# First tile of a split-GELU multiply: two contiguous blocks of four adjacent rows a partition

## Chip, cores, metric

One core of one Trainium2 chip. The metric is the device time of one execution in microseconds (us). Before: 469.24 us, median of 3 runs (469.23 to 469.35).

## The reference

```python
def setup_inputs():
    batch, seq, dim = (32, 512, 2048)
    return {'x': np.random.randn(batch, seq, dim).astype(np.float32)}

def reference(x):
    half_dim = x.shape[-1] // 2
    x1, x2 = x[..., :half_dim], x[..., half_dim:]          # copies cut
    gelu_x1 = 0.5 * x1 * (1 + erf(x1 / np.sqrt(2)))
    return (gelu_x1 * x2).astype(np.float32)
```

That is 16,384 rows of 8 KiB in and of 4 KiB out: 134.22 MB read and 67.11 MB written.

## The kernel before

Sixteen tiles of 1024 rows. In each, a partition holds eight adjacent rows (64 KiB in, 32 KiB out). There are two input and two output buffers. SP (SyncE) issues the loads, ACT (ScalarE) does the GELU and issues most stores, DVE (VectorE) multiplies. The first tile is loaded, and the first and last tiles are stored, in two halves of four rows a partition.

```python
    R = 8
    x_t = x_flat.rearrange("(n p r) d -> n p r d", p=P, r=R)
    o_t = out_flat.rearrange("(n p r) d -> n p r d", p=P, r=R)
    # ... buffers and semaphores cut ...
    def load(i, rows, sem):
        ins = nc.sync.dma_start(out=x_bufs[i % 2][:, rows, :], in_=x_t[i][:, rows, :])
        counted(ins, sem, 16)
        return ins

    def store(queue, i, rows, sem):
        queue.wait_ge(mul_done, n[mul_done.name])
        counted(
            queue.dma_start(out=o_t[i][:, rows, :], in_=o_bufs[i % 2][:, rows, :]), sem, 16
        )

    for ins in (
        load(0, slice(0, 4), first[0]),
        load(0, slice(4, 8), first[1]),
        load(1, slice(0, 8), ready[1]),
    ):
        tc.no_tile_sem_insts.add(ins.ins.name)
    # ... for each tile i (cut): wait for its load and for the store that frees its output buffer,
    #     GELU and multiply in pieces, store, then load(i + 2)
```

## Time and profile before

| | before |
|---|---|
| time, median of 3 | 469.24 us |
| span of the profiled run | 467.9 us |
| DVE / ACT busy | 140.5 us (30%) / 115.5 us (25%) |
| two DMA queues, share of 16 engines | 70.6% + 29.1% |

The prediction below shows most of the profile lines. In addition, these are lines of the page's list of DMA issues: what is copied, the issuing queue, how often, KB each, and the median us from issue to landing.

```profile
x_tile<-in_x_dram SPq DMA_DIRECT2D x2, 4096.0 KB, 16.6
out_dram<-o_tile ACTq DMA_DIRECT2D x2, 2048.0 KB, 34.5
...
x_tile<-in_x_dram SPq DMA_DIRECT2D x15, 44.2
```

The first line is the two half loads, the second the two half stores of the first tile. The times to landing hold the waiting behind other transfers on the same sixteen DMA engines. "DMA engine" here is always one of those sixteen. The trace records each packet that they move, with start, duration and size, but not which engine moved it: a packet is put on the engine whose packet before it ends as it starts. That gives each of the sixteen the same 120 loads of 64 KiB.

### The profile page before, as it was taken

To read this page: it belongs to the slowest core of one execution; us is meant where nothing else is said; L and a number is where in the kernel's file an instruction comes from. 1 tells how busy PE (TensorE), PEld (TensorE's weight loads), DVE (VectorE), ACT (ScalarE), POOL (GpSimd) and SP (SyncE) were. 2 spreads that over 40 slices of the span, in tenths; PEclk is the share of its full clock that TensorE was granted. 3 is DMA by queue.
4 is the path that set the end of the run, shared out by engine and by line. 5 is a ranking of instruction groups with operands and counts; after the bars stand their busy time and mean duration, and the time that the engine had idled before them with its cause. 6 is when DMAs were issued, how large, how long until landed. Compare 5 with 4: busy or idle time off the path is not lost.

```text
span 467.9 us, 152 instructions
## 1 busy us (share of the span) xinstructions
DVE 140.5 (30%) x34; ACT 115.5 (25%) x35; POOL 0.2 (0%) x4
## 2 busy tenths in 40 slices
DVE  0330514207052060511606116060150702507043
ACT  1320606042060410604106050050500506014060
POOL 0000000000000000000000000000000000000000
DMA  8999999999999999999999999999999999999998
GB/s 359 448 448 443 403 405 492 409 403 448 459 437 403 434 417 493 403 403 448 476 420 403 445 406 493 403 406 445 487 409 403 445 451 448 403 434 417 493 389 373
DMA packets 5041, 201.34 MB, mean 430 GB/s; under 512 B 560, under 2 KB 560, under 8 KB 560
## 3 DMA queue, kind: packets, MB, share of 16 engines
q1 hardware_dynamic: 2880, 142.61, 70.6%
q10 hardware_dynamic: 2160, 58.72, 29.1%
q14 instruction: 1, 0.01, 0.0%
HBM read 134.22 MB, written 67.11 MB: 430 GB/s over the span
## 4 chain that ended last, share of the span: by engine, by line
DMA 76%; DVE 14%; ACT 8%; ACTq 0%; SPq 0%; issue 0%
DMA out_dram<-o_tile 66%; DVE o_tile L89 14%; DMA x_tile<-in_x_dram 10%; ACT o_tile L81 8%; ACTq L112 0%; SPq L47 0%
## 5 line engine op out<-in xcount | busy, mean ns | idle before, releaser
L89 DVE TENSOR_TENSOR o_tile<-o_tile,x_tile 128x5120 f32<-128x5120 f32 (+3 forms) x34 | 140.5, 4171 | 319.7 <-ACT o_tile L81 319.7
L81 ACT ACTIVATE o_tile<-x_tile 128x5120 f32<-128x5120 f32 (+3 forms) x34 | 114.3, 3407 | 337.4 <-DMA out_dram<-o_tile 301.6
L81 ACT ACT_TABLE_LOAD x1 | 1.3, 1283 | 2.9 <-PEq L67 2.9
L135 POOL MEMSET const-bfloat16-1.0<- 128x1 bf16 x1 | 0.1, 101 | 0.0
L135 POOL MEMSET const-uint8-127<- 128x1 uint8 x1 | 0.1, 101 | 0.0
L135 POOL MEMSET const-float32-0.0<- 128x1 f32 x1 | 0.1, 98 | 0.2 <-issue 0.2
L135 POOL MEMSET const-float32-1.0<- 128x1 f32 x1 | 0.1, 98 | 0.0
## 6 DMA issues: line engine op xcount, KB each, us to landing
out_dram<-o_tile ACTq DMA_DIRECT2D x13, 4096.0 KB, 44.7
x_tile<-in_x_dram SPq DMA_DIRECT2D x2, 4096.0 KB, 16.6
out_dram<-o_tile ACTq DMA_DIRECT2D x2, 2048.0 KB, 34.5
out_dram<-o_tile SPq DMA_DIRECT2D x1, 4096.0 KB, 25.2
out_dram<-o_tile SPq DMA_DIRECT2D x2, 2048.0 KB, 7.8
x_tile<-in_x_dram SPq DMA_DIRECT2D x15, 44.2
```

Of the source, the lines that this page charges most:

```text
L81: nc.scalar.activation(out=o_bufs[k][:, rows, :], in_=x_bufs[k][:, rows, :half], func=GELU),
L89: nc.vector.tensor_mul(out=o_bufs[k][:, rows, :], in0=o_bufs[k][:, rows, :], in1=x_bufs[k][:, rows, half:],),
L135: nc = _bacc.Bacc("TRN2", target_bir_lowering=False, num_devices=1)
```

## The change

In the old form, a half load takes every second 32 KiB of the first tile's 8 MiB, and a half store every second 16 KiB of its 4 MiB. The new form gives partition p of half h the four rows from 4p on in block h, so that each half is one contiguous piece of memory. The intent is longer contiguous runs for the transfers that stand at the kernel's start. Nothing else changes.

```diff
+    x_h = x_t[0].rearrange("p r d -> (p r) d").rearrange("(h p r) d -> h p r d", h=2, p=P)
+    o_h = o_t[0].rearrange("p r d -> (p r) d").rearrange("(h p r) d -> h p r d", h=2, p=P)
     def load(i, rows, sem):
-        ins = nc.sync.dma_start(out=x_bufs[i % 2][:, rows, :], in_=x_t[i][:, rows, :])
+        src = x_h[rows.start // 4] if i == 0 else x_t[i][:, rows, :]
+        ins = nc.sync.dma_start(out=x_bufs[i % 2][:, rows, :], in_=src)
     def store(queue, i, rows, sem):
         queue.wait_ge(mul_done, n[mul_done.name])
-        counted(
-            queue.dma_start(out=o_t[i][:, rows, :], in_=o_bufs[i % 2][:, rows, :]), sem, 16
-        )
+        dst = o_h[rows.start // 4] if i == 0 else o_t[i][:, rows, :]
+        counted(queue.dma_start(out=dst, in_=o_bufs[i % 2][:, rows, :]), sem, 16)
```

## The prediction

> **What bounds the kernel now.** I read the page first (engine shares, DMA row, queues), then the chain of work that ended last in order of time, then the table of stretches over the first 21 us, then the single DMA packets that the trace records.
>
> The page: no compute engine is busy for a third of the span, and the DMA row is full from slice 2 to slice 39.
>
> ```profile
> span 467.9 us, 152 instructions
> DVE 140.5 (30%) x34; ACT 115.5 (25%) x35; POOL 0.2 (0%) x4
> DMA  8999999999999999999999999999999999999998
> DMA packets 5041, 201.34 MB, mean 430 GB/s; under 512 B 560, under 2 KB 560, under 8 KB 560
> q1 hardware_dynamic: 2880, 142.61, 70.6%
> q10 hardware_dynamic: 2160, 58.72, 29.1%
> HBM read 134.22 MB, written 67.11 MB: 430 GB/s over the span
> ```
>
> The two queues together hold 70.6 + 29.1 = 99.7% of sixteen engines' span. There are 17 loads and 18 stores, 35 transfers; 560 = 35 x 16 packets are the tiny completion writes, so 5041 - 560 - 1 = 4480 = 35 x 128 carry data: **one packet for each partition of each transfer**. Their sizes in the packet records: on q1 384 of 32 KiB (256 of the two half loads of the first tile, the rest of one whole store), 1920 of 64 KiB (the 15 whole loads) and 256 of 16 KiB (the last tile's half stores), and on q10 256 of 16 KiB (the two half stores of the first tile) and 1664 of 32 KiB (13 whole stores).
>
> The chain of waits confirms it from the other side: 76% of it is DMA, and its pieces are a transfer of some 44.7 us, an ACT and two DVE instructions, and a transfer again. Its start is one uninterrupted load piece:
>
> ```profile
> 1.59 0.05 issue
> 1.64 45.54 DMA x_tile<-in_x_dram
> 47.18 0.02 issue
> 47.20 4.48 ACT o_tile L81
> 51.68 0.02 issue
> 51.70 8.77 DVE o_tile L89 x2
> 60.48 0.02 issue
> 60.50 40.04 DMA out_dram<-o_tile
> ```
>
> The chain shows ACT and DVE for 13.3 us of each round, but the DMA row stays at 9 during them, since the next load is queued then. So I don't take that 13.3 us for a loss: the bound is the sixteen DMA engines, from their first packet to their last.
>
> The table of stretches for the part that the change touches (start up to the first packets' end; first half load; second half load):
>
> ```profile
> core 0: us, DVE busy (x) ACT busy (x) POOL busy (x), PEclk, DMA share, GB/s
> 0.00:3.40 3.40, 0.00 (x0) 0.54 (x1) 0.20 (x4) 1.00 0.54 154
> 3.40:11.90 8.50, 0.00 (x0) 0.74 (x1) 0.00 (x0) 1.00 1.00 432
> 11.90:21.55 9.65, 4.49 (x2) 3.71 (x2) 0.00 (x0) 1.00 1.01 435
> ```
>
> The gapped half loads already run at 432 and 435 GB/s, with a DMA share of 1.00 and 1.01. There is no idle time in them to win.
>
> **What the Trainium skill says.** (1) "DMA: Bandwidth & Descriptors", section "Where 436 GB/s comes from", puts the ceiling of the sixteen ports at 435 GB/s. The trace agrees: 432 and 435 GB/s in the two half loads. (2) "Perfetto Trace Analysis", section "Contiguity and DMAs": contiguity "only matters within an SBUF partition line". In both kernels each partition gets 32 KiB in one piece from memory. The trace agrees that a gap costs nothing: the gapped 32 KiB load packets take 1213 ns (median; 27.0 GB/s on one engine), and 64 KiB packets of the whole loads, which leave no gaps, take 2418 ns (27.1 GB/s). (3) "DMA: Bandwidth & Descriptors", section "Latency and other measured facts", reports loss from power-of-two row pitches of 512 KiB and more. The change takes the load pitch from 64 KiB to 32 KiB and the store pitch from 32 to 16 KiB, all below that; no run here has such a large pitch. (4) Same page, section "Why a DMA increments its semaphore by 16 and not by 1": the number of engines comes from the slowest dimension of both patterns, 128 partitions giving 16. The trace agrees: every transfer has 16 completion writes.
>
> **The change part by part.**
>
> *Removed and added:* nothing is counted differently. Two half loads of 4 MiB, two half stores of 2 MiB, the same six ACT and DVE instructions on the same shapes, the same waits. Only DRAM addresses move: partition p of half h takes rows 4p to 4p+3 of block h in place of half of its own eight rows.
>
> *Number and size of packets:* the whole stores of the kernel before are of just the new form (128 partitions, 32 KiB each, no gaps in memory), and the packet records show 128 packets of 32 KiB for each. I take it that the new half loads become 128 packets of 32 KiB and the new half stores 128 of 16 KiB, as now.
>
> *Cost of a packet:* load, 32 KiB: starts on one engine are 1209 to 1210 ns apart, back to back. 8 packets an engine and half, 2 halves: 16 x 1.21 = 19.4 us. Store, 16 KiB: 611 ns each, 16 x 0.611 = 9.8 us. In all the change touches 29.1 us of each engine's 465 us, **6%**. To move the total by 2% (9.4 us), these packets would have to become a third faster or slower. A third faster is not to be had, as they run at the rate of all the others.
>
> *What could still change:* I chained the packets of each engine by time and added up what each took above the median of its size. Over the whole kernel this is 1.0 us an engine, and only in two places: about 0.61 us in the first packets (1596 to 1985 ns in place of 1213, starting at 1.74 to 2.30 us), and 0.33 us at 21.6 to 30 us, where the second tile's load begins (2538 to 2942 ns in place of 2418). After 50 us it is 0.00 to 0.02 in every 10 us. The first is the cold start of sixteen streams, which a contiguous source does not take away: the first packet of each engine is contiguous already. The second belongs to the next tile's load, which the change leaves alone. I give the pair an expected change of 0, with a swing of some 0.3 us either way. As the engines are backlogged from 1.74 to 467 us, any such change carries through to the end one to one.
>
> *Beside other work:* the compute of the first tile (ACT 7.3 us, DVE 8.9 us) lies wholly beside loads and keeps its landing times of about 12.7 and 22.4 us.
>
> Sum: 469.24 + 0.0 (packets) + 0.0 (compute) + 0.0 (start) = **469.2 us**.
>
> **Rivals.**
>
> *The gap in memory costs something that the change recovers* (fewer open pages, longer runs). For: the first packets are slow. Against: from the second packet on, gapped and ungapped packets have the same rate within 0.4%, and in the stretch table the half loads stand at the kernel's own ceiling. At most the 0.6 us of the cold start plus the 0.3 us of the transition could vanish: 468.3 us. Chance of more than 0.4 us gained: 6%.
>
> *The smaller pitch makes the engines collide in memory.* Sixteen engines start within 0.6 us of each other, now at half the distance in memory. If the first loads ran 10% slower, that is 1.9 us: 471.1 us. Against: whole stores go at this very pitch of 32 KiB with 1213 ns a packet. Chance of more than 0.4 us lost: 7%.
>
> *The contiguous region is cut into other descriptors or given to fewer engines* (a region with no gaps could be folded into one long run). On one engine 4 MiB would take 128 x 1.21 = 155 us, and the kernel would be well over 100 us slower; with more, smaller packets on sixteen engines, the effect would be below 1 us. Against: whole loads and whole stores are free of gaps too, and are spread over sixteen engines with one packet a partition. Chance of a visible loss: under 1%.
>
> **Range and chances.** The three runs before lie within 0.12 us. To that I add the swing of 0.3 us and a little for another chip's session: **468.9 to 469.6 us**. The rivals on either side leave about 6% below and 8% above, and somewhat more for the unknown. Faster by over 2% (under 460.0 us) has no mechanism: 0.004. Slower by over 2% (over 478.8 us) only by the third rival: 0.006. Within 2%: 0.99.
>
> **What would show each step right or wrong.** Right: 5041 packets and 201.34 MB again; 560 tiny ones; 32 KiB load packets at 1213 ns after each engine's first, and 16 KiB store packets at 611 ns; half loads landing near 12.7 and 22.4 us; 430 to 436 GB/s in the stretches 3.4 to 11.9 and 11.9 to 21.55 us; chain and waits as before. Wrong: another count of packets (third rival), 32 KiB packets over 1250 ns in the first 22 us (second rival), first packets near 1213 ns or the second tile's first packets near 2418 ns with a total of 468.3 to 468.8 us (first rival). A change of the later 44.7 us pieces would refute the claim that nothing beyond the first tile is touched.

## The result, and the profile after

Six executions of the changed kernel: 469.14, 469.29, **471.70**, 469.28, **471.37**, 469.16 us. The median is 469.28. Six of the kernel before: 469.23 to 469.35, median 469.30. The ratio is 1.0015 (95% interval 0.9991 to 1.0038). Ratios here are the mean time of one kernel's runs over that of the other's of the same rounds, so not quite the ratio of the medians. Executions over 1.5% slower than the fastest of the same kernel are left out of the means. The mean of the six is 470.0 us, as two of them took 2.2 and 2.5 us longer than the others.

The profiled execution is one of the short ones (469.14 us). Its page, the lines that answer to those of before:

```profile
span 467.8 us, 152 instructions
DMA  8999999999999999999999999999999999999988
DMA packets 5041, 201.34 MB, mean 430 GB/s; under 512 B 560, under 2 KB 560, under 8 KB 560
q1 hardware_dynamic: 2880, 142.61, 70.6%
q10 hardware_dynamic: 2160, 58.72, 29.1%
...
x_tile<-in_x_dram SPq DMA_DIRECT2D x2, 4096.0 KB, 16.9
out_dram<-o_tile ACTq DMA_DIRECT2D x2, 2048.0 KB, 34.1
...
x_tile<-in_x_dram SPq DMA_DIRECT2D x15, 44.4
```

The same packets and the same bytes. The half loads land 0.3 us later (16.9 for 16.6). Its table of stretches:

```profile
core 0: us, DVE busy (x) ACT busy (x) POOL busy (x), PEclk, DMA share, GB/s
0.00:3.40 3.40, 0.00 (x0) 0.54 (x1) 0.20 (x4) 1.00 0.56 154
3.40:11.90 8.50, 0.00 (x0) 0.74 (x1) 0.00 (x0) 1.00 1.00 432
11.90:21.55 9.65, 4.50 (x2) 3.71 (x2) 0.00 (x0) 1.00 1.01 435
```

The contiguous half loads run at 432 and 435 GB/s, to the digit as the gapped ones did (a stretch counts the packets that start in it, so a shift of some 0.1 us does not show). The start of its chain of waits:

```profile
1.64 45.34 DMA x_tile<-in_x_dram
46.99 0.02 issue
47.01 4.48 ACT o_tile L84
```

The first piece ends 0.19 us sooner (46.99 for 47.18), although the half loads landed later. So a short execution is much as predicted. It has nothing to say about the two long ones, whose traces were not kept.

### The profile page after: what moved, and what is told of

Read it like the earlier page. It is cut to its first block, busy times and chain, and to the rows that moved or that the text cites. A ratio compares the mean times of both kernels' runs of the same rounds, so it can differ in the third digit from the quotient of the medians.

```text
span 467.8 us, 152 instructions
## 1 busy us (share of the span) xinstructions
DVE 140.5 (30%) x34; ACT 115.5 (25%) x35; POOL 0.2 (0%) x4
## 2 busy tenths in 40 slices
DMA packets 5041, 201.34 MB, mean 430 GB/s; under 512 B 560, under 2 KB 560, under 8 KB 560
## 4 chain that ended last, share of the span: by engine, by line
DMA 76%; DVE 14%; ACT 8%; ACTq 0%; SPq 0%; issue 0%
DMA out_dram<-o_tile 66%; DVE o_tile L92 14%; DMA x_tile<-in_x_dram 10%; ACT o_tile L84 8%; ACTq L115 0%; SPq L51 0%
## 6 DMA issues: line engine op xcount, KB each, us to landing
x_tile<-in_x_dram SPq DMA_DIRECT2D x2, 4096.0 KB, 16.9
```

## The experiments

Theory A: the contiguous first tile brings the long executions. Theory B: they fall on any kernel, and the first rounds missed them on the old one. Theory C came with the traces: a DMA engine out of step with the others falls further behind. "One-turn" kernels do the work once.

### Both kernels again, and each half of the change alone

The first two are unedited. The other two are the changed kernel with one of its two addresses put back (wrong in the first 1024 rows):

```diff
# loads_only
-        dst = o_h[rows.start // 4] if i == 0 else o_t[i][:, rows, :]
+        dst = o_t[i][:, rows, :]
# stores_only
-        src = x_h[rows.start // 4] if i == 0 else x_t[i][:, rows, :]
+        src = x_t[i][:, rows, :]
```

> The kernel before, unchanged, as a run of its own. Theory A (the contiguous first tile itself brings executions of about 471.5 us, seen in 2 of 6 runs of the changed kernel and in 0 of 6 of the kernel before): all of these runs and of the shared runs of the kernel before lie at 469.2 to 469.4. Theory B (such executions happen to either kernel, and the first rounds missed them by chance): some of the ten lie at 471 to 472.

> The changed kernel, unchanged. Theory A: one to three of the runs at 471 to 472, the others at 469.1 to 469.3. Theory B: the same share as the kernel before on this chip, perhaps none. If the profiled execution is a slow one, its trace should have some 2.2 us of idle DMA engines, or packets longer than 2418 ns for 64 KiB, that the fast trace lacks.

> Half loads contiguous, half stores at the old addresses; the first 1024 rows come out permuted, so the result is wrong on purpose. Theory A1 (the loads bring the slow executions, by shifting the start): one to three of five at 471 to 472. Theory A2 (the stores bring them): all at 469.1 to 469.3. Theory B: as the kernel before.

> Half stores contiguous, half loads at the old addresses; wrong on purpose in the first 1024 rows. Theory A1: all at 469.2 to 469.4. Theory A2: one to three of five at 471 to 472. Theory B: as the kernel before.

Measured: before 469.25 to 469.43, after 469.19 to 469.33, loads only 469.17 to 469.32, stores only 469.18 to 469.55 us; the shared runs of the kernel before 469.13 to 469.51. No long execution among twenty-nine. Theory A's one to three of five came neither in the changed kernel nor with the loads alone, but nothing is told apart: the event is too rare for five executions. The same kernel twice more:

> The changed kernel once more, five more executions against five or more of the kernel before. Theory A: one or more of five at 471 to 472 us. Theory B (a rare event that falls on any kernel): most likely none, 469.1 to 469.4 us.

> The changed kernel once more, for the count of slow executions: theory A one or more of five at 471 to 472 us; theory B most likely none, all at 469.1 to 469.4 us.

469.09 to 469.25 and 469.12 to 469.32 us: none again.

### Does a gap in memory cost anything? All sixteen tiles in halves

Every load and store becomes two halves, in the old form in one kernel and in the new form in the other. They differ in two lines:

```diff
# gapped_all to contig_all
-                out=x_bufs[i % 2][:, half_rows, :], in_=x_t[i][:, half_rows, :]
+                out=x_bufs[i % 2][:, half_rows, :], in_=x_h[i][h]
-                queue.dma_start(out=o_t[i][:, half_rows, :], in_=o_bufs[i % 2][:, half_rows, :]),
+                queue.dma_start(out=o_h[i][h], in_=o_bufs[i % 2][:, half_rows, :]),
```

> The old form of the first tile given to all sixteen tiles: each load and each store is two halves, and each half takes every second 32 KiB (loads) or 16 KiB (stores) of the tile's memory. Against the run beside it with contiguous halves, any cost of a gap is sixteen times that in the first tile. Theory 'a gap costs nothing': packets 1213 ns and 611 ns, 469.2 to 469.6 us, as the run beside it within 0.3 us. Rival 'a gap costs, and the first tile was too little to show it': slower than the run beside it by more than 1 us.

> The new form given to all sixteen tiles: each half load and half store is one contiguous block. Theory 'a gap costs nothing': 469.2 to 469.6 us. Rival: over 1 us less than the gapped run beside it. Theory A (contiguous halves bring the executions of 471.5 us): more of them here than the 2 in 6, as there are sixteen times as many such halves.

Measured: 470.86 us gapped (470.81 to 471.28), 470.87 us contiguous (470.70 to 471.07). The gap costs nothing with sixteen times as many gapped loads. Theory A's guess for the contiguous kernel, more long executions than 2 in 6, failed: its five lie within 0.4 us of each other. Both are 1.5 us above the kernel before, which I had not expected. The packet records give most of it: on one engine, two 32 KiB packets take 2 x 1209 ns from start to start where one of 64 KiB takes 2414, two stores of 16 KiB 2 x 607 where one of 32 KiB takes 1209. With 120 such load packets and 112 such store packets an engine that is 0.5 + 0.6 us, and 464 more completion writes add 29 x 6 ns = 0.2 us an engine.

### Can addresses matter at all? Pieces 1 MiB apart

```diff
-    x_t = x_flat.rearrange("(n p r) d -> n p r d", p=P, r=R)
-    o_t = out_flat.rearrange("(n p r) d -> n p r d", p=P, r=R)
+    x_t = x_flat.rearrange("(p n r) d -> n p r d", p=P, r=R)
+    o_t = out_flat.rearrange("(p n r) d -> n p r d", p=P, r=R)
```

> The other way round: partition p holds rows 128p to 128p+127, so that the pieces of a transfer lie 1 MiB apart for loads and 512 KiB apart for stores; the result stays right. It tells whether the distance of the pieces in memory can matter here at all. If the 16 engines are the bound whatever the addresses: 469 to 470 us and packets of 2418 ns. If engines in step collide at such a pitch, as the skill's page on DMA reports for pitches of 512 KiB and more: packets clearly longer than 2418 ns and a total over 500 us.

Five executions of 510.30 to 515.25 us (a sixth took 523.56), 1.094 times the kernel before. Its packets are as many and as large; 64 KiB packets take up to 4701 ns. From its page, and from its table of stretches (columns as above):

```profile
DMA packets 5041, 201.34 MB, mean 396 GB/s; under 512 B 560, under 2 KB 560, under 8 KB 560
```

```profile
50.00:400.00 350.00, 96.37 (x22) 80.96 (x23) 0.00 (x0) 1.00 1.00 403
```

The DMA engines are as full (share 1.00) and move 403 GB/s, where the kernel before moves 432 in that stretch. So a full DMA row does not prove that addresses are harmless; at pitches of 32 and 64 KiB they are, at 1 MiB for loads and 512 KiB for stores they are not. The Trainium skill, "DMA: Bandwidth & Descriptors", section "Latency and other measured facts", reports such a loss, for copies between tensors in HBM (the chip's main memory): 207 GB/s at a pitch of 512 KiB and 164 at 2 MiB, for 214 at full rate. These runs agree with the direction.

### Sixteen turns in one launch

One trace shows one execution, so a rare event has to be given more chances. The whole work is repeated sixteen times; a turn begins when the last stores of the turn before have landed.

```diff
-    for i in range(n_tiles):
+    for turn in range(16):
+        if turn:
+            nc.sync.wait_ge(tail_stored, n[tail_stored.name])
+            nc.scalar.wait_ge(tail_stored, n[tail_stored.name])
+            load(0, slice(0, 4), first[0])
+            load(0, slice(4, 8), first[1])
+            load(1, slice(0, 8), ready[1])
+        for i in range(n_tiles):           # body as before, one level deeper
-                nc.scalar.wait_ge(first[lo // 4], 16)
+                nc.scalar.wait_ge(first[lo // 4], 16 * (turn + 1))
```

> The whole work of the kernel before done sixteen times in one launch, each turn begun when the last stores of the turn before have landed; the result is right. One trace then holds sixteen turns, and five timed executions hold eighty. A turn should take some 467 us, the whole 7470 to 7500 us. Theory A (only the contiguous first tile brings turns 2.2 us longer): no turn over 1 us longer than the median turn, and the executions within 1 us of each other. Theory B (a rare event on any kernel): the turns and executions scatter as those of the changed kernel do, by multiples of some 2 us.

> The same for the changed kernel. Theory A: at 2 slow ones in 16 executions so far, about two of sixteen turns in the trace 2.2 us longer than the median turn, and the trace shows there where the DMA engines stand idle or take longer; the executions scatter by several us. Theory B: turns alike, and the same mean turn as the kernel before within 0.1 us. If the slow executions come once in a launch and not in a turn (something at its start), neither kernel shows them within the turns.

> Sixteen turns, contiguous half loads with the old half stores (wrong on purpose in the first 1024 rows). Theory A1 (the loads make slow turns likelier): 7483 to 7487 us as the changed kernel's sixteen turns, two or more slow turns in the trace. Theory A2 (the stores do): 7478 to 7481 us as the kernel before. Theory B (neither does): between the two without order.

> Sixteen turns, contiguous half stores with the old half loads (wrong on purpose in the first 1024 rows). Theory A1: 7478 to 7481 us, at most one slow turn in the trace. Theory A2: 7483 to 7487 us, two or more slow turns. Theory B: without order.

The last two have the change for loads alone and for stores alone. The first two kernels ran on one chip in the same rounds, the last two on another. In the traces a turn, from its first load's issue to its last store's landing, takes 466.8 to 467.8 us or 469.3 to 470.3 us, nothing between:

| kernel | first tile's loads | six executions, us | mean | long turns in the trace |
|---|---|---|---|---|
| before_x16 | gapped | 7478.22 to 7480.99 | 7480.2 | 1 of 16 |
| stores_x16 | gapped | 7478.17 to 7482.64 | 7480.2 | 0 of 16 |
| after_x16 | contiguous | 7483.67 to 7486.87 | 7484.5 | 2 of 16 |
| loads_x16 | contiguous | 7478.98 to 7486.36 | 7483.4 | 4 of 16 |

**Where a long turn loses its time.** The last stretch of turns 6 and 7 of the changed kernel, in the table of stretches, at the same distance from each turn's start. First the short turn 6, then the long turn 7:

```profile
core 0: us, DVE busy (x) ACT busy (x) POOL busy (x), PEclk, DMA share, GB/s
2784.20:2796.90 12.70, 5.65 (x3) 7.22 (x3) 0.00 (x0) 1.00 0.90 390
2796.90:2799.20 2.30, 2.30 (x1) 0.00 (x0) 0.00 (x0) 1.00 0.91 392
2799.20:2807.60 8.40, 0.97 (x1) 0.00 (x0) 0.00 (x0) 1.00 0.87 373
```

```profile
3251.70:3264.40 12.70, 3.74 (x2) 5.68 (x3) 0.00 (x0) 1.00 0.96 415
3264.40:3266.70 2.30, 1.49 (x2) 1.53 (x1) 0.00 (x0) 1.00 0.45 192
3266.70:3278.00 11.30, 3.69 (x1) 0.00 (x0) 0.00 (x0) 1.00 0.80 338
```

Some 457 us into the long turn the DMA share falls to 0.45: the engines have little left to move, since ACT began the last tile 451.0 us into the turn and not 448.3, and its half stores are not issued yet. These are its lines in the two turns, which began at 2340.16 and 2807.69 us:

```profile
2788.49 7.22 ACT L92 ACTIVATE o_tile<-x_tile 128x2048 f32<-128x2048 f32 x3 [21.86 <-DMA out_dram<-o_tile]
3258.72 7.22 ACT L92 ACTIVATE o_tile<-x_tile 128x2048 f32<-128x2048 f32 x3 [21.88 <-DMA out_dram<-o_tile]
```

Why the last tile came late is seen in the packets. Each engine moves one 64 KiB load packet a round. For each round this gives the median start of the sixteen packets, how far behind it the latest one starts, and how long that one takes. It is worked out from the packet records of turn 7:

```
round  median start  latest behind by  latest took (ns)  median took (ns)
  0      21.22 us        0.45 us           2567              2530
  3      30.43           0.59              2601              2433
  4      33.47           0.75              2548              2418
  5      36.49           0.89              2738              2418
  6      39.52           1.20              2898              2428
  7      42.57           1.66              2706              2469
  8      45.66           1.89              2871              2596
  9      48.87           2.14              2418              2456
 14      64.05           2.07              2418              2418
```

One engine starts 0.45 us behind and takes longer than the others round after round. It stays some 2.1 us behind up to round 17, falls back once more there, and ends the turn 2.8 us behind. In turn 6 the latest is 0.31 us behind in round 0, 0.17 us in round 9 and 0.8 us at the end. The sixteen share the work evenly (120 load packets each), so the last one sets when the last tile can start, and so the end. This holds in all seven sixteen-turn traces of this document, those further down included: in the last round the latest engine is 2.2 to 3.8 us behind in all 29 long turns, and at most 0.9 us in all 83 short ones.

**What starts it.** The seven long turns in these traces have one of two beginnings. In four (turn 7 of after_x16, turns 3, 7 and 10 of loads_x16) the latest engine is 0.45 to 0.49 us behind the median in round 0. In three (turn 2 of before_x16, turn 2 of after_x16, turn 12 of loads_x16) one engine gets an 8 KiB instruction fetch of 309 ns between its load packets, and falls back from there. Most fetches do nothing: each of the four traces holds twelve in its turns, and at most one of them begins a long turn.

**What the contiguous loads change.** Over the 32 turns with gapped loads and the 32 with contiguous loads:

| first tile's loads | first packets, mean ns | next tile's load begins | its first packets, mean ns | latest engine behind, mean | turns with it 0.40 us or more behind |
|---|---|---|---|---|---|
| gapped | 1787 | 21.13 us | 2742 | 0.247 us | 0 of 32 |
| contiguous | 1862 | 21.23 us | 2560 | 0.313 us | 7 of 32 |

Contiguous loads start 75 ns slower and leave the engines further apart. Of the seven turns with 0.40 us or more, four became long (three at 0.41, 0.44 and 0.46 us did not). Leaving out the three turns begun by a fetch, contiguous loads have 4 long turns of 32 and gapped loads none. This points to theory A1, that the loads do it. Four turns against none is still a split that chance alone gives about once in eighteen; the seven against none with 0.40 us or more, about once in 180. On the other side, the next tile's first packets are 182 ns shorter, more than the 95 ns by which they begin later: this fits the short executions of the changed kernel, whose mean in all its one-turn runs is 469.21 us (19 runs) for 469.32 us of the kernel before (64 runs).

### Putting one engine out of step on purpose

First attempt: 8 KiB more, issued by GpSimd when the first tile's product is done.

```diff
+    nc.gpsimd.wait_ge(mul_done, 3)
+    nc.gpsimd.dma_start(out=spare[0:1, :], in_=x_flat[0:1, :]).then_inc(nudged, 16)
```

> The kernel before, with one more DMA of 8 KiB into one partition, which runs on one DMA engine alone, issued at 30.5 us, when the first tile's last product is there. Theory C (an engine that falls some 0.3 us out of step with the others meets slow packets until it is one packet behind): all or many executions at 471.5 to 472.5 us, and the trace has one engine with packets of 2600 to 3350 ns after the nudge and some 1 us of idle time on the other 15 near 457 us. Rival D (a delay costs just itself): 469.4 to 469.8 us, and no such packets.

> The same nudge in the changed kernel. Theory C: 471.5 to 472.5 us in many executions. Rival D: 469.3 to 469.7 us. If the new addresses matter to it (theory A), more of these executions are slow than with the nudge in the kernel before.

469.29 to 469.74 us, and 469.17 to 469.41 with one at 471.53 us. The queues of the profile of the kernel before with the nudge show why this tests nothing:

```profile
q0 software_dynamic: 32, 0.01, 0.0%
```

32 packets: the transfer was cut into 16 of 512 bytes, 27 ns each, one on every engine, with 16 completion writes. No engine was put out of step.

Second attempt: a prime number of elements, which can't be cut evenly, issued by SP between the second half load and the next tile's load, in each of sixteen turns. The element count is 2039 (8156 bytes) or 4051 (16,204 bytes).

```diff
+    def lag():
+        ins = nc.sync.dma_start(
+            out=spare[0:1, :], in_=x_flat[0:2, :].rearrange("a b -> (a b)")[None, 0:4051]
+        )
+        counted(ins, lagged, 16)
+        return ins
             load(0, slice(4, 8), first[1])
+            nc.sync.wait_ge(lagged, n[lagged.name])
+            lag()
             load(1, slice(0, 8), ready[1])
```

> Sixteen turns of the kernel before; in each, one DMA engine alone gets 8 KiB more (some 0.3 us) between the second half load and the next tile's load, at about 21.5 us. Theory C (a lag of one engine sets it off): many of the sixteen turns 2 to 3 us longer, 7495 to 7525 us. Rival D (the lag costs itself): 16 x 0.3 = 5 us at most over 7478 to 7481, so 7478 to 7486 us, with at most one or two slow turns in the trace.

> The same with 16 KiB, some 0.6 us, on the one engine. Theory C: more slow turns than with 0.3 us, 7500 to 7530 us. Rival D: 16 x 0.6 = 10 us at most over 7478 to 7481, so 7478 to 7491 us.

> The same 0.3 us in the changed kernel. Theory C: 7495 to 7525 us, and if the new addresses make an engine easier to set off, more slow turns than in the kernel before with the same lag. Rival D: 7478 to 7490 us.

The packet records show one packet of the full size in each turn, 308 and 605 ns.

| kernel | extra on one engine | six executions, us | mean | long turns in the trace |
|---|---|---|---|---|
| before_x16 | none | 7478.22 to 7480.99 | 7480.2 | 1 of 16 |
| before_lag03_x16 | 0.31 us a turn | 7481.76 to 7487.78 | 7485.6 | 3 of 16 |
| before_lag06_x16 | 0.61 us a turn | 7510.78 to 7518.03 | 7514.8 | **16 of 16** |
| after_lag03_x16 | 0.31 us a turn | 7485.02 to 7495.62 | 7489.5 | 3 of 16 |

With 0.61 us on one engine the *old* kernel, gapped loads and all, is long in every turn: (7514.8 - 7480.2) / 16 = 2.2 us a turn, over three times the delay put in. (The two ran on different chips, but the one-turn kernel before took 469.30 and 469.31 us on average beside them.) In each turn the engine that got the extra packet is the latest, in round 0 and in the last round. In its first turn the latest engine is 0.54, 0.87, 1.13, 1.54, 1.80 and 2.16 us behind in rounds 0 to 5, and stays at 2.15 until round 16. Rival D, that a delay costs just itself, allowed 7491 us at most. So theory C holds for 0.6 us. With 0.31 us it missed: 3 long turns of 16 in each trace, one of them begun by a fetch, and means within rival D's ranges (up to 7486 and 7490 us), not at theory C's 7495 and more. But rival D's account does not fit either: a short turn with the extra packet takes 467.29 and 467.22 us on average in the two traces, for 467.26 and 467.23 without it, so the delay is then absorbed. The smaller lag is not enough by itself.

## Why the prediction was right or wrong

- **The bound, right.** The sixteen DMA engines are full from start to end in every one-turn execution traced, all of them short.
- **The packets, right.** 5041 packets, 201.34 MB, the same sizes; 1213 and 611 ns; 432 and 435 GB/s in the half loads. The third rival (other descriptors) is out.
- **A gap costs nothing, right.** 470.86 against 470.87 us with every tile in halves.
- **The second rival, as put, wrong.** Packets after the first are no slower at the smaller pitch. The first ones are, by 75 ns, and leave the engines further apart. Its guess of 1.9 us comes near the size of the long executions, through another mechanism.
- **The first rival, nearly nothing.** The cold start stays. The 0.33 us at the next tile's start, which the prediction said the change leaves alone, shrinks by some 0.18 us, and the short executions gain 0.11 us on average.
- **The step that failed:** "I give the pair an expected change of 0, with a swing of some 0.3 us either way. As the engines are backlogged from 1.74 to 467 us, any such change carries through to the end one to one." It took the sixteen engines for one, and looked at their mean. In the runs 0.61 us on one engine became 2.2 us of time, and with the contiguous start an engine is 0.45 us or more out of step in 4 long turns of 32. That would be the tail at 471.4 to 471.7 us (untraced, see below), which the range of 468.9 to 469.6 did not hold. The range was drawn from the spread of three executions (0.12 us), which can't show an event of this rarity. That two of the first six were long was partly luck: of the 26 later one-turn executions with contiguous loads that are counted below, one was.

How sure is theory A? Of the one-turn runs (without those of all tiles in halves), long executions number 3 of 32 with contiguous loads (two of the changed kernel's 21, none of 5 with loads only, one of 6 with the nudge) and 0 of 74 with gapped loads. Sixteen-turn means are 3.2 and 4.3 us higher with contiguous loads, 0.2 to 0.27 us a turn. Chance alone gives a split like 3 of 32 against 0 of 74 about once in 39. These and the traces agree, but one turn of the old kernel was long too, begun by a fetch, and with 0.61 us on one engine all its turns are. (The traces of the changed kernel and of the kernel before that do the work once have one fetch in the span, at 460 to 461 us, near the end.) So theory B has its part: the event belongs to both kernels, and the change, very likely, makes it more frequent.

**Left open.** The two long executions of the first rounds were not traced; that they are long turns is argued from their size (2.2 and 2.5 us over the mean of the other four). Why an engine out of step meets slower packets, why it stops two to four us behind, and why a contiguous start is 75 ns slower, no run shows. A version that beats both kernels did not come up: the short executions of the change gain 0.02%, which its long ones take back (mean of 21 runs 469.43 us, against 469.32).

## What to carry to other kernels

Where each partition's piece is already contiguous and large, making the whole transfer contiguous bought nothing here (pitches of 16 to 64 KiB); check with the rate in the stretch, not with the shape of the addresses. Where all DMA engines are full, read them one by one: a delay of one engine of 0.6 us at the start cost over three times that at the end. And take the range of a prediction from more than three executions, as rare long ones are part of a kernel's time.

## What the Trainium skill lacked or had wrong

- "DMA: Bandwidth & Descriptors" (no section has it): 0.61 us more on one of sixteen full engines cost 2.2 us a turn, as that engine's 64 KiB packets then took 2.7 to 3.1 us for 2.42 (rounds 0 to 4 of the first turn) and it ended the turns 2.2 to 3.8 us behind.
- The same page, section "Latency and other measured facts": its loss for large power-of-two pitches is given for copies between HBM tensors, from 512 KiB up. It was seen here in loads and stores of SBUF (the on-chip memory that holds the tiles) too: 403 GB/s for 432 with 1 MiB for loads and 512 KiB for stores. The page has no smaller pitch; at 32 and 64 KiB for loads there was no loss (432 to 435 GB/s).
- "Runtime: NRT & Kernel Launch", section "Instruction fetch mechanics", has no figure for what a fetch costs a DMA-bound kernel: here it was one 8 KiB packet of 309 ns on one of the engines that move the data, which began three of the seven long turns.
